# The expert loop of a two-layer MoE trunk: engine order written out by hand, gated values turned earlier, three overflow blocks taken into the loop

## The chip, the cores and the metric

The kernel runs on one core of one Trainium2 chip. The metric is the device time of one execution in microseconds (us). A core has TensorE (PE, matmuls; PEld is its weight load), VectorE (DVE), ScalarE (ACT), GpSimd (POOL) and SyncE (SP, which here issues DMAs), and 16 DMA engines that the queues of all engines share. Each engine takes its instructions strictly in the order of its own list; between engines there are semaphores.

## The reference, cut to what matters

The program has two layers. Each layer has attention and a recurrent mix, and then a mixture of experts: every token picks one of four groups and two of eight experts in it. Of the 1024 tokens, 2048 (token, expert) pairs go to 32 experts, in blocks of 128 rows of one expert.

```python
def block_mlp(args):
    tok, e = args
    xb = h_pad[tok]
    hid = jax.nn.silu(xb @ w_gate[e]) * (xb @ w_up[e])
    return hid @ w_down[e]

yb = lax.map(block_mlp, (row_tok.reshape(n_blocks, ROW_BLOCK), block_e))
y = jax.ops.segment_sum(yb.reshape(R, D) * row_w[:, None], row_tok, num_segments=T + 1)
```

D is 1024 and an expert is 256 wide. All is float32.

## The kernel before, in words

A layer ends with the expert stage, `moe`. Expert e has a fixed block of 128 slots, whose tokens stand in the tables `idx_g` (which row to gather) and `idx_s` (where to scatter); `wsl` holds the weights of the slots. Tokens beyond 128 of one expert go to up to 15 overflow blocks, which `route_overflow` numbers at run time: `ovf` holds how many there are and whose expert each is. With these inputs each layer has three.

For one expert the steps are:

- `gather` (L1595): an indirect DMA, issued by POOL, brings the block's rows from `h2d` into `xg`, of which there are two.
- `transposed` (L1603): eight PE transposes turn them into `xT_ps`; `prepare` splits that into `xT_hi` (ACT, L1611) and `xT_lo` (DVE, L1612), whose sum is the float32 value.
- `load_gu` brings the gate and up weights from HBM in two halves of 1 MB into five buffers `w_gu`; `split_half` splits each half into `w_hi` (ACT, L1580) and `w_lo` (DVE, L1581), three pairs of buffers. `load_d` brings `w_d`, 1 MB, three buffers. All these loads are issued by SP, in order.
- `up` (L1628 to L1630): 24 matmuls into `h_ps`; `hidden` makes the gated values `th` (ACT tanh L1618, DVE L1619 and L1620).
- `down`: two PE transposes turn `th` into `hT_ps` (L1649), a DVE copy brings them back (L1651), four float32 matmuls make `y_ps` (L1655; the profile has each as two), DVE scales them into `yo` (L1658; one buffer), and POOL issues an indirect DMA that scatters `yo` into `yd` (L1659).

`down` of expert e-1 is written behind `up` of e, so that its inputs are ready. The order on each engine is not the order of the code: a scheduler lays the instructions out by the dependencies and its own estimates of time, engine by engine.

After the 32 experts come the overflow blocks, each inside a nested `If` on the count: `prepare_late` and `up_late` (L1642) take the float32 weights without a split, with half as many, slower matmuls. After the last scatter the next layer (or the end) reads `yd` back.

Of the kernel before, what the change touches and what calls it, by code (L numbers as in the profile page):

```python
# [52 lines left out]
class Trunk:  # L53
# [1436 lines left out]
    def route_overflow(self, w, psum):  # L1490
# [83 lines left out]

    def split_half(self, n, eng=None):

        nc = self.nc
        raw = self.raw[n % 5]
        lo, hi = self.parts[n % 3]
        nc.scalar.copy(hi, raw)  # L1580
        (eng or nc.vector).tensor_tensor(lo, raw, hi.bitcast(F32), op=OP.subtract)  # L1581

    def moe(self, l, side, psum):

        nc, tc = self.nc, self.tc
        with ExitStack() as s:
# [28 lines left out]
            def hidden(ph):  # L1615
                x = tx.tile([128, 512], F32, name="th", tag="mt")
                th = x[:, 0:256]
# [3 lines left out]
                return x  # L1621

            def up(e, x):
                hi, lo = x
                ph = psum.tile([128, 512], F32, name="h_ps", tag="h", bufs=2)
                for k in range(NK):
                    wlo, whi = self.parts[(2 * e + k // 4) % 3]
# [3 lines left out]
                return hidden(ph)  # L1631

            def prepare_late(e):
                pt = transposed(e)
                nc.scalar.copy(late[e % 2], pt)
                return late[e % 2]

            def up_late(e, x):

                ph = psum.tile([128, 512], F32, name="h_ps", tag="h", bufs=2)  # L1640
                for k in range(NK):
                    nc.tensor.matmul(ph, x[:, k, :], self.raw[(2 * e + k // 4) % 5][:, k % 4, :], start=(k == 0), stop=(k == NK - 1))  # L1642
                return hidden(ph)

            def down(e, th):
                w = self.wd[e % 3]
                pt = psum.tile([128, 2, 128], F32, name="hT_ps", tag="hT", bufs=1)
                for k in range(2):
                    nc.tensor.transpose(pt[:, k, :], th[:, 128 * k:128 * k + 128], self.ident)  # L1649
                hT = th[:, 256:512].rearrange("p (a b) -> p a b", a=2)  # L1650
                nc.vector.tensor_copy(hT, pt)  # L1651
                po = psum.tile([128, D], F32, name="y_ps", tag="y", bufs=1)
                for half in range(2):
                    for k in range(2):
                        nc.tensor.matmul(po[:, 512 * half:512 * half + 512], hT[:, k, :], w[:, k, 512 * half:512 * half + 512],  # L1655
                                         start=(k == 0), stop=(k == 1))
                yo = tx.tile([128, D], F32, name="yo", tag="x", bufs=1)
                nc.vector.scalar_tensor_tensor(yo, po, self.wsl[:, e:e + 1], gt2, op0=OP.mult, op1=OP.mult)  # L1658
                st = nc.gpsimd.indirect_dma_start(out=self.yd, out_offset=bass.IndirectOffsetOnAxis(ap=self.idx_s[:, e:e + 1], axis=0),  # L1659
                                                  in_=yo, in_offset=None, bounds_check=2 * T - 1, oob_is_err=False)  # L1660
                for o in scat:
                    tc.declare_no_dep(st.ins, o.ins, reason="every slot holds another row")
                scat.append(st)
# [242 lines left out]
```

## Time and profile before

| | us |
|---|---|
| median of 3 runs (2875.5 to 2880.1) | 2878.36 |
| the profiled execution | 2890.55 |
| its span, first to last instruction | 2888.7 |
| PE matmuls busy in the span | 2452.3 (85%) |
| DVE busy | 1845.5 (64%) |
| ACT busy | 1063.5 (37%) |
| POOL busy | 721.3 (25%) |

A window over one turn of the loop tells how much of it each engine works; the timeline gives every instruction's start and duration, with the idle time of its engine before it and what ended that; the DMA views count the packets of a queue in a stretch of time (q0 holds what POOL issues: the gathers and scatters; q1 the loads of SP). PEclk is the share of TensorE's clock that was granted: 1.00 is 2.4 GHz, 0.50 is 1.2 GHz.

### The profile page before, as it was taken

What the parts mean: (1) busy time and instruction counts of PE and PEld (TensorE: products, weight loads), DVE (VectorE), ACT (ScalarE), POOL (GpSimd) and SP (SyncE); (2) the same over time, 40 slices, a digit from 0 to 9 for tenths busy, and PEclk for the clock granted to TensorE, in tenths of its full rate; (3) what the DMA queues carried; (4) which work ended last, traced back from release to release, by engine and by line L of the source; (5) the groups of instructions that cost most, each with busy time, mean ns of one, the idle gap of its engine ahead of it and who ended that gap; (6) DMA issues with size and microseconds to landing.
All of it is one profiled execution on the core that took longest, in us unless ns stands there. A gap on an engine that the chain in (4) does not pass through costs nothing.

```text
span 2888.7 us, 45371 instructions
## 1 busy us (share of the span) xinstructions
PE 2452.3 (85%) x17281; PEld 1842.3 (64%) x17281; DVE 1845.5 (64%) x3927; ACT 1063.5 (37%) x1908; POOL 721.3 (25%) x569
## 2 busy tenths in 40 slices
PE   5999987998789779999849888889877986999991
PEld 3766666787678656666427666778756775666650
DVE  5358785555684767767264689756467566776745
ACT  3333332343463224444133343334345331444421
POOL 4122232222420511111141222221242032111113
PEclk8989998998899779999969989899889986999996
DMA  8477575452442359899551434453443224998874
GB/s 285 157 233 215 178 239 135 134 147 93 161 127 93 140 190 328 312 329 336 188 203 52 136 122 140 151 155 115 127 158 114 98 100 147 342 350 317 306 261 186
DMA packets 264230, 548.99 MB, mean 190 GB/s; under 512 B 77048, under 2 KB 181440, under 8 KB 233280
## 3 DMA queue, kind: packets, MB, share of 16 engines
q1 hardware_dynamic: 235424, 490.90, 50.6%
q0 software_dynamic: 23952, 40.99, 3.9%
q10 hardware_dynamic: 4624, 14.06, 1.2%
q8 instruction: 141, 2.31, 0.3%
q14 instruction: 89, 0.73, 0.1%
HBM read 467.68 MB, written 120.09 MB: 203 GB/s over the span
## 4 chain that ended last, share of the span: by engine, by line
PE 52%; DVE 23%; DMA 11%; ACT 7%; issue 5%; POOL 1%; SPq 1%; DVEq 0%; ACTq 0%; POOLq 0%
PE y_ps L1655 8%; PE pj L335 5%; PE pj L336 5%; PE pj L337 5%; DVE w_lo L1581 4%; ACT w_hi L1580 4%; PE h_ps L1629 3%; PE h_ps L1628 2%; DVE sv_m L724 2%; DVE sv_t L726 2%; PE h_ps L1630 2%; PE po L1284 2%; DMA ada_w<-in_ada_w 2%; DMA yd<-yo,idx_s 2%; PE po L1285 2%
## 5 line engine op out<-in xcount | busy, mean ns | idle before, releaser
L1581 DVE TENSOR_TENSOR w_lo<-w_gu,w_hi 128x2048 fp32r<-128x2048 f32 x122 | 279.6, 2292 | 206.3 <-ACT w_hi L1580 202.1
L1580 ACT CAST w_hi<-w_gu 128x2048 fp32r<-128x2048 f32 x128 | 244.0, 1908 | 384.6 <-PE h_ps L1629 367.4
L335 PE MATMUL pj<-hh,wa_hi 128*128 128x512 f32 x800 | 341.6, 427 | 2.7 <-ACT wa_hi L322 1.9
L336 PE MATMUL pj<-hl,wa_hi 128*128 128x512 f32 x800 | 332.0, 415 | 1.1 <-DVE hl L312 1.1
L337 PE MATMUL pj<-hh,wa_lo 128*128 128x512 f32 x800 | 328.9, 413 | 3.3 <-POOL wa_lo L323 3.3
L1655 PE MATMUL y_ps<-w_d,th 128*128 128x512 f32 x560 | 260.3, 608 | 40.9 <-DVE th L1651 25.5
L1628 PE MATMUL h_ps<-w_hi,xT_hi 128*128 128x512 f32 x512 | 225.8, 441 | 3.9 <-ACT xT_hi L1611 3.9
L1629 PE MATMUL h_ps<-w_hi,xT_lo 128*128 128x512 f32 x512 | 210.8, 412 | 2.6 <-DVE xT_lo L1612 2.6
L1630 PE MATMUL h_ps<-w_lo,xT_hi 128*128 128x512 f32 x512 | 203.2, 397 | 0.0
L1655 PEld LDWEIGHTS y_ps<-w_d,th 128*128 128x128 f32 x560 | 101.3, 190 | 156.9 <-issue 103.3
L323 POOL TENSOR_TENSOR wa_lo<-wa_raw,wa_hi 128x1024 fp32r<-128x1024 f32 x50 | 122.0, 2441 | 315.6 <-ACT wa_hi L322 262.0
L335 PEld LDWEIGHTS pj<-hh,wa_hi 128*128 128x128 f32 x800 | 157.8, 197 | 42.0 <-issue 7.4
L337 PEld LDWEIGHTS pj<-hh,wa_lo 128*128 128x128 f32 x800 | 156.8, 196 | 39.5 <-POOL wa_lo L323 4.6
L336 PEld LDWEIGHTS pj<-hl,wa_hi 128*128 128x128 f32 x800 | 157.8, 197 | 37.2 <-issue 4.5
L1659 POOL DMA_INDIRECT yd<-yo,idx_s x70 | 70.5, 1008 | 402.2 <-DVE yo L1658 323.6
L1595 POOL DMA_INDIRECT xg<-h2d,idx_g x74 | 80.1, 1082 | 299.2 <-PE hT_ps L1649 250.7
L1629 PEld LDWEIGHTS h_ps<-w_hi,xT_lo 128*128 128x128 f32 x512 | 98.2, 192 | 50.5 <-DVE xT_lo L1612 30.9
L1658 DVE SCALAR_TENSOR_TENSOR yo<-y_ps,wsl,gt 128x1024 f32<-128x1024 f32 x70 | 89.5, 1279 | 52.2 <-PE y_ps L1655 27.0
L1628 PEld LDWEIGHTS h_ps<-w_hi,xT_hi 128*128 128x128 f32 x512 | 98.4, 192 | 36.7 <-issue 12.9
L724 DVE TENSOR_TENSOR sv_m<-sv_t,sv_n 64x31 f32<-64x31 f32 (+15 forms) x248 | 104.5, 421 | 23.0 <-DMA sv_n<-sp_z 18.5
L1154 ACT ACTIVATE at_p<-at_s,at_mx 128x256 f32<-128x256 f32 (+7 forms) x128 | 94.9, 742 | 63.7 <-DVE at_mx L1152 63.2
L1152 DVE TENSOR_REDUCE at_mx<-at_s 128x1 f32<-128x256 f32 (+7 forms) x128 | 95.8, 753 | 31.3 <-PE at_s L1150 30.4
(438 smaller groups left out, 5428.7 us busy)
## 6 DMA issues: line engine op xcount, KB each, us to landing
w_gu<-in_moe_w_gu SPq DMA_DIRECT2D x144, 1024.0 KB
w_d<-in_moe_w_down SPq DMA_DIRECT2D x72, 1024.0 KB
ada_w<-in_ada_w SPq DMA_DIRECT2D x80, 512.0 KB
wa_raw<-in_w_in SPq DMA_DIRECT2D x50, 512.0 KB
sp_z<-z SPq DMA_DIRECT2D x32, 768.0 KB
b_zz<-sp_z SPq DMA_DIRECT2D x32, 512.0 KB
cy<-yd SPq DMA_DIRECT2D x16, 1024.0 KB
qkv<-qst SPq DMA_DIRECT2D x48, 256.0 KB
```

Source lines behind the costliest of these rows:

```text
L323: nc.gpsimd.tensor_tensor(lo, raw, hi.bitcast(F32), op=OP.subtract)
L335: nc.tensor.matmul(ps, hi[:, k, :], self.hh[k][:, sl], start=(k == 0), stop=False)
L336: nc.tensor.matmul(ps, hi[:, k, :], self.hl[k][:, sl], start=False, stop=False)
L337: nc.tensor.matmul(ps, lo[:, k, :], self.hh[k][:, sl], start=False, stop=(k == NK - 1))
L724: eng.tensor_tensor(t3, tt[:, 0:j + 1, j].unsqueeze(2).to_broadcast([64, j + 1, 31 - j]), nt[:, j, j + 1:32].unsqueeze(1).to_broadcast([64 ...
L1152: nc.vector.tensor_reduce(mx, ps[:, 0:n], axis=AX.X, op=OP.max, negate=True)
L1580: nc.scalar.copy(hi, raw)
L1581: (eng or nc.vector).tensor_tensor(lo, raw, hi.bitcast(F32), op=OP.subtract)
L1628: nc.tensor.matmul(ph, hi[:, k, :], whi[:, k % 4, :], start=(k == 0), stop=False)
L1629: nc.tensor.matmul(ph, lo[:, k, :], whi[:, k % 4, :], start=False, stop=False)
L1630: nc.tensor.matmul(ph, hi[:, k, :], wlo[:, k % 4, :], start=False, stop=(k == NK - 1))
L1655: nc.tensor.matmul(po[:, 512 * half:512 * half + 512], hT[:, k, :], w[:, k, 512 * half:512 * half + 512], start=(k == 0), stop=(k == 1))
```

## The change

The loop runs over N = 35 blocks: 32 experts and the first three overflow blocks, whose expert SP reads from `ovf`; they are split like the others. Only the fourth and later overflow blocks stay in `If`s.

The loop is written in two pieces, and a new `in_order` ties every instruction of PE, ACT, DVE and POOL in them to the one before it on its engine. So the code's order is the engines' order. SP is left out of it.

The turning of `th` is a step of its own, `turned`. It stands ahead of the transposes of the next expert's rows, and its copy is on ACT, into a tile `hT` of its own. The scatter of e-1 is written ahead of the gather of e+2.

`route_overflow` and the late blocks take their scratch tile from one that an earlier stage (`sg`) uses, `load_gu` loads one half a call, and the buffers of the halves are numbered through.

```diff
+    MORE_E = 3
...
+    @contextmanager
+    def in_order(self, last):
+
+        engines = [e.engine for e in (self.nc.tensor, self.nc.scalar, self.nc.vector, self.nc.gpsimd)]
+        traced = self.nc.cur_bb.bb.instructions
+        n = len(traced)
+        yield
+        for i in traced[n:]:
+            if i.engine in engines:
+                if i.engine in last:
+                    self.tc.add_manual_dep(i, last[i.engine].name, mybir.DependencyInfo(mybir.DependencyClass.NoSync, mybir.DependencyReason.DATA),
+                                           reason="program order")
+                last[i.engine] = i
...
-    def load_gu(self, l, i, e):
-
-        for half in range(2):
-            self.nc.sync.dma_start(self.raw[(2 * i + half) % 5], self.expert_source(l, e, "moe_w_gu")[half])
+    def load_gu(self, l, n, e):
+
+        self.nc.sync.dma_start(self.raw[n % self.RAW], self.expert_source(l, e, "moe_w_gu")[n % 2])
...
-            def down(e, th):
-                w = self.wd[e % 3]
+            def turned(e):
                 pt = psum.tile([128, 2, 128], F32, name="hT_ps", tag="hT", bufs=1)
                 for k in range(2):
-                    nc.tensor.transpose(pt[:, k, :], th[:, 128 * k:128 * k + 128], self.ident)
-                hT = th[:, 256:512].rearrange("p (a b) -> p a b", a=2)
-                nc.vector.tensor_copy(hT, pt)
+                    nc.tensor.transpose(pt[:, k, :], ths[:, e % 2, 128 * k:128 * k + 128], self.ident)
+                nc.scalar.copy(hT, pt)
...
             gather(0)
             gather(1)
-            x, prev = prepare(0), None
-            for e in range(32):
-                th = up(e, x)
-                for n in (2 * e + 3, 2 * e + 4):
-                    if n < 64:
-                        self.split_half(n)
-                if e + 1 < 32:
-                    if e + 2 < 32:
-                        gather(e + 2)
-                    x = prepare(e + 1)
+            x, last = prepare(0), {}
+            for e in range(N):
+                with self.in_order(last):
+                    ph = up(e, x)
+                    if e + 1 < N:
+                        self.split_half(2 * e + 3)
+                    if e:
+                        turned(e - 1)
+                    if e + 1 < N:
+                        x = prepare(e + 1)
+                    hidden(e, ph)
                 if e == 0:
                     nc.sync.dma_start(gt2, self.mod_row(l, 5).partition_broadcast(128))
-                if prev is not None:
-                    down(*prev)
-                prev = (e, th)
-                if e < 28:
-                    self.load_gu(l, e + 4, e + 4)
-                if 0 < e < 30:
-                    self.load_d(l, e + 2, e + 2)
+                with self.in_order(last):
+                    if e:
+                        down(e - 1)
+                        scatter(e - 1)
+                    if e + 2 < N:
+                        gather(e + 2)
+                        self.split_half(2 * e + 4)
+                for n in (2 * e + 8, 2 * e + 9):
+                    if n < 2 * N:
+                        self.load_gu(l, n, expert(n // 2))
+                if e and e + 2 < N:
+                    self.load_d(l, e + 2, expert(e + 2))
                 if e == 2:
                     self.route_overflow(xp, psum)
-                if e == 29:
-                    self.load_gu(l, 32, block_weights(0))
...
+            turned(N - 1)
+            down(N - 1)
+            scatter(N - 1)
...
             with ExitStack() as ifs:
-                for b in range(15):
+                for b in range(self.MORE_E, 15):
                     ifs.enter_context(tc.If(n > b))
...
```

What this does to the engines' lists shows best on POOL, at the start of layer 0's loop, from the first gather on. `xg0` and `xg1` are the two row buffers, so the gathers alternate between them; a row with `yd0` is a scatter. Before:

```order
L1595 DMA xg0_10477<-h2d0_614,idx_g_10451 128x1024
L1595 DMA xg1_10478<-h2d0_614,idx_g_10451 128x1024
L1595 DMA xg0_10477<-h2d0_614,idx_g_10451 128x1024
L1595 DMA xg1_10478<-h2d0_614,idx_g_10451 128x1024
L1595 DMA xg0_10477<-h2d0_614,idx_g_10451 128x1024
L1659 DMA yd0_615<-yo_10610,idx_s_10450 2048x1024
L1595 DMA xg1_10478<-h2d0_614,idx_g_10451 128x1024
L1659 DMA yd0_615<-yo_10676,idx_s_10450 2048x1024
L1595 DMA xg0_10477<-h2d0_614,idx_g_10451 128x1024
```

And now, the same place on POOL:

```order
L1614 DMA xg0_10477<-h2d0_614,idx_g_10451 128x1024
L1614 DMA xg1_10478<-h2d0_614,idx_g_10451 128x1024
L1614 DMA xg0_10477<-h2d0_614,idx_g_10451 128x1024
L1676 DMA yd0_615<-yo_10605,idx_s_10450 2048x1024
L1614 DMA xg1_10478<-h2d0_614,idx_g_10451 128x1024
L1676 DMA yd0_615<-yo_10670,idx_s_10450 2048x1024
L1614 DMA xg0_10477<-h2d0_614,idx_g_10451 128x1024
L1676 DMA yd0_615<-yo_10827,idx_s_10450 2048x1024
L1614 DMA xg1_10478<-h2d0_614,idx_g_10451 128x1024
```

Five gathers stood ahead of the first scatter, and now three: each gather has moved behind two scatters.

On PE, between two experts in the middle of the loop (the last of one `h_ps`, the turnings, `y_ps`, the first of the next `h_ps`), before:

```order
L1629 MATMUL h_ps_11899<-w_hi2_10323,xT_lo_11879 128x512
L1630 MATMUL h_ps_11899<-w_lo2_10322,xT_hi_11878 128x512
L1603 MATMUL xT_ps_11935<-ident_86,xg1_10478 128x128 x8
L1649 MATMUL hT_ps_11948<-ident_86,th_11858 128x128 x2
L1655 MATMUL y_ps_11952<-w_d1_10469,th_11858 128x512 x4
L1628 MATMUL h_ps_11965<-w_hi0_10327,xT_hi_11944 128x512
```

The same place on PE now:

```order
L1647 MATMUL h_ps_11880<-w_hi2_10326,xT_lo_11856 128x512
L1648 MATMUL h_ps_11880<-w_lo2_10327,xT_hi_11855 128x512
L1666 MATMUL hT_ps_11907<-ident_86,th_10481 128x128 x2
L1622 MATMUL xT_ps_11911<-ident_86,xg1_10478 128x128 x8
L1687 MATMUL y_ps_11927<-w_d1_10469,hT_10482 128x512 x4
L1646 MATMUL h_ps_11945<-w_hi0_10322,xT_hi_11920 128x512
```

The two turnings have changed places; `y_ps` stands behind both, as before.

On DVE, from one scaling of `y_ps` to the next, before:

```order
L1658 SCALAR_TENSOR_TENSOR yo<-y_ps,wsl,gt_10476 128x1024
L1581 TENSOR_TENSOR w_lo_10322<-w_gu_10330,w_hi_10323 128x2048
L1651 COPY th<-hT_ps 128x256
L1581 TENSOR_TENSOR w_lo_10326<-w_gu_9795,w_hi_10327 128x2048
L1619 SCALAR_TENSOR_TENSOR th<-th,h_ps 128x256
L1612 TENSOR_TENSOR xT_lo<-xT_ps,xT_hi 128x1024
L1620 TENSOR_TENSOR th<-th,h_ps 128x256
L1658 SCALAR_TENSOR_TENSOR yo<-y_ps,wsl,gt_10476 128x1024
```

And now:

```order
L1673 SCALAR_TENSOR_TENSOR yo<-y_ps,wsl,gt_10476 128x1024
L1595 TENSOR_TENSOR w_lo_10325<-w_gu_10329,w_hi_10324 128x2048
L1595 TENSOR_TENSOR w_lo_10327<-w_gu_10330,w_hi_10326 128x2048
L1631 TENSOR_TENSOR xT_lo<-xT_ps,xT_hi 128x1024
L1637 SCALAR_TENSOR_TENSOR th<-th,h_ps 128x256
L1638 TENSOR_TENSOR th<-th,h_ps 128x256
L1673 SCALAR_TENSOR_TENSOR yo<-y_ps,wsl,gt_10476 128x1024
```

The copy between the two `w_lo` is gone from DVE, and `xT_lo` stands ahead of both steps of `th`.

## Rows read from the trace of the kernel before

**Rows 1.** The page's chain that ended last, by line: shares of the span.

```profile
PE y_ps L1655 8%; PE pj L335 5%; PE pj L336 5%; PE pj L337 5%; DVE w_lo L1581 4%; ACT w_hi L1580 4%; PE h_ps L1629 3%; PE h_ps L1628 2%; DVE sv_m L724 2%; DVE sv_t L726 2%; PE h_ps L1630 2%; PE po L1284 2%; DMA ada_w<-in_ada_w 2%; DMA yd<-yo,idx_s 2%; PE po L1285 2%
```

**Rows 2.** Window, one turn: length, busy PE PEld DVE ACT POOL, PEclk, DMA share, GB/s.

```profile
1261.27:1272.34 11.07, 10.45 (x44) 7.02 (x43) 7.91 (x8) 5.00 (x4) 2.08 (x2) 1.00 0.89 304
```

**Rows 3.** Timeline, that turn: start, duration, instruction, [idle before <-what ended it].

```profile
1261.30 0.79 PE L1628 MATMUL h_ps<-w_hi,xT_hi 128*128 128x512 f32 x1
...
1267.35 1.03 PE L1603 MATMUL xT_ps<-ident,xg 128*128 128x128 f32 x8
...
1268.66 1.07 POOL L1595 DMA_INDIRECT xg<-h2d,idx_g  x1 [3.90 <-PE hT_ps L1649]
...
1269.23 3.70 PE L1655 MATMUL y_ps<-w_d,th 128*128 128x512 f32 x8 [0.62 <-DVE th L1651]
1269.26 2.29 DVE L1581 TENSOR_TENSOR w_lo<-w_gu,w_hi 128x2048 fp32r<-128x2048 f32 x1
...
1274.82 1.01 POOL L1659 DMA_INDIRECT yd<-yo,idx_s  x1 [5.09 <-DVE yo L1658]
```

**Rows 4.** Timeline, the ends of both layers' expert stages.

```profile
1034.22 0.79 PE L1628 MATMUL h_ps<-w_hi,xT_hi 128*128 128x512 f32 x1
...
1058.21 3.70 PE L1655 MATMUL y_ps<-w_d,th 128*128 128x512 f32 x8 [0.38 <-DVE th L1651]
...
1438.21 3.70 PE L1655 MATMUL y_ps<-w_d,th 128*128 128x512 f32 x8 [0.52 <-DVE th L1651]
...
2427.10 0.80 PE L1628 MATMUL h_ps<-w_hi,xT_hi 128*128 128x512 f32 x1
...
2827.61 3.70 PE L1655 MATMUL y_ps<-w_d,th 128*128 128x512 f32 x8 [0.52 <-DVE th L1651]
```

**Rows 5.** Timeline, overflow blocks of layer 0.

```profile
1412.28 3.70 PE L1655 MATMUL y_ps<-w_d,th 128*128 128x512 f32 x8 [0.52 <-DVE th L1651]
...
1416.02 1.28 DVE L1658 SCALAR_TENSOR_TENSOR yo<-y_ps,wsl,gt 128x1024 f32<-128x1024 f32 x1 [3.79 <-PE y_ps L1655]
1417.58 0.99 POOL L1659 DMA_INDIRECT yd<-yo,idx_s  x1 [9.67 <-DVE yo L1658]
1418.88 1.03 POOL L1595 DMA_INDIRECT xg<-h2d,idx_g  x1 [0.31 <-issue]
1419.44 0.33 SPq L1570 DMA_DIRECT2D w_gu<-in_moe_w_gu  x1
1419.97 0.33 SPq L1573 DMA_DIRECT2D w_d<-in_moe_w_down  x1
...
1431.85 1.03 POOL L1595 DMA_INDIRECT xg<-h2d,idx_g  x1 [0.31 <-issue]
```

**Rows 6.** DMA queue q0 from 1432.9 to 1434: packets, MB, share of 16 engines.

```profile
q0 software_dynamic: 144, 0.00, 5.7%
```

**Rows 7.** Timeline, two more gathers and a `y_ps` behind a wait.

```profile
1025.89 1.92 POOL L1595 DMA_INDIRECT xg<-h2d,idx_g  x1 [0.30 <-issue]
...
1397.61 5.40 PE L1655 MATMUL y_ps<-w_d,th 128*128 128x512 f32 x8 [3.48 <-DVE th L1651]
...
1406.87 1.04 POOL L1595 DMA_INDIRECT xg<-h2d,idx_g  x1 [0.30 <-issue]
```

**Rows 8.** DMA queue q0 from 1024.0 to 1031.2.

```profile
q0 software_dynamic: 288, 0.80, 38.8%
```

**Rows 9.** DMA queue q0 from 1422.4 to 1424.6.

```profile
q0 software_dynamic: 144, 0.00, 3.7%
```

**Rows 10.** DMA queue q0 from 1410.9 to 1415.0.

```profile
q0 software_dynamic: 144, 0.02, 2.9%
```

**Rows 11.** Windows: length, busy PE PEld DVE ACT POOL, PEclk, DMA share, GB/s.

```profile
1043.40:1046.70 3.30, 1.59 (x10) 1.06 (x8) 3.03 (x3) 2.61 (x3) 1.03 (x1) 1.00 0.37 84
1046.80:1053.50 6.70, 5.27 (x13) 4.17 (x14) 2.54 (x6) 0.00 (x0) 0.00 (x0) 0.50 0.68 273
...
1398.30:1401.70 3.40, 3.40 (x6) 1.33 (x5) 0.00 (x0) 0.00 (x0) 0.20 (x1) 0.50 0.99 366
```

More of the change, by code (lines that the diff above doesn't have):

```diff
@@ L1556, in first_tiles @@
         self.wd = [wp.tile([128, 2, D], F32, name="w_d0")]
+    RAW = 5
     def more_tiles(self, wp):
-        self.parts = [[wp.tile([128, 4, 512], F32R, name=f"w_{n}{i}") for n in ("lo", "hi")] for i in (2, 1, 0)][::-1]
-        self.raw += [wp.tile([128, 4, 512], F32, name=f"w_gu{i}") for i in range(2, 5)]
+        self.parts = [[wp.tile([128, 4, 512], F32R, name=f"w_{n}{i}") for n in ("hi", "lo")] for i in range(3)]
+        self.raw += [wp.tile([128, 4, 512], F32, name=f"w_gu{i}") for i in range(2, self.RAW)]
     def expert_source(self, l, e, n):
@@ L1591, in moe @@
                 nc.gpsimd.memset(x, 0.0)
+            ths = tx.tile([128, 2, 256], F32, name="th", tag="mt")
+            hT = tx.tile([128, 2, 128], F32, name="hT", tag="mt")
             scat = []
@@ L1641, in up_late, with scaled, scatter, down @@
                 for k in range(NK):
-                    nc.tensor.matmul(ph, x[:, k, :], self.raw[(2 * e + k // 4) % 5][:, k % 4, :], start=(k == 0), stop=(k == NK - 1))
-                return hidden(ph)
-            def down(e, th):
-                w = self.wd[e % 3]
+                    nc.tensor.matmul(ph, x[:, k, :], self.raw[(2 * e + k // 4) % self.RAW][:, k % 4, :], start=(k == 0), stop=(k == NK - 1))
+                hidden(e, ph)
+            def turned(e):
                 pt = psum.tile([128, 2, 128], F32, name="hT_ps", tag="hT", bufs=1)
                 for k in range(2):
-                    nc.tensor.transpose(pt[:, k, :], th[:, 128 * k:128 * k + 128], self.ident)
-                hT = th[:, 256:512].rearrange("p (a b) -> p a b", a=2)
-                nc.vector.tensor_copy(hT, pt)
+                    nc.tensor.transpose(pt[:, k, :], ths[:, e % 2, 128 * k:128 * k + 128], self.ident)
+                nc.scalar.copy(hT, pt)
+            yos = {}
+            def scaled(e, po):
+                yo = yos[e] = tx.tile([128, D], F32, name="yo", tag="x", bufs=1)
+                nc.vector.scalar_tensor_tensor(yo, po, self.wsl[:, e:e + 1], gt2, op0=OP.mult, op1=OP.mult)
+            def scatter(e):
+                st = nc.gpsimd.indirect_dma_start(out=self.yd, out_offset=bass.IndirectOffsetOnAxis(ap=self.idx_s[:, e:e + 1], axis=0),
+                                                  in_=yos.pop(e), in_offset=None, bounds_check=2 * T - 1, oob_is_err=False)
+                for o in scat:
+                    tc.declare_no_dep(st.ins, o.ins, reason="every slot holds another row")
+                scat.append(st)
+            def down(e):
+                w = self.wd[e % 3]
                 po = psum.tile([128, D], F32, name="y_ps", tag="y", bufs=1)
@@ L1656, in down @@
                                          start=(k == 0), stop=(k == 1))
[L1657 to L1663, printed above, removed]
+                scaled(e, po)
             def block_weights(b):
@@ L1705, in moe @@
+            down(N - 1)
+            scatter(N - 1)
+            late = self.lay.tile([128, 8, 128], F32, name="xT", tag="sg")
             n = nc.values_load(self.ovf[0:1, 0:1], min_val=0, max_val=15)
             with ExitStack() as ifs:
[L1707 removed]
+                for b in range(self.MORE_E, 15):
                     ifs.enter_context(tc.If(n > b))
[L1709 to L1710 removed]
+                    if b == self.MORE_E:
+                        gather(32 + b)
+                        overflow(b)
+                    x = prepare_late(32 + b)
@@ L1711, in moe @@
                     if b + 1 < 15:
+                        gather(33 + b)
                         overflow(b + 1)
-                    down(32 + b, up_late(32 + b, x))
-                    if b + 1 < 15:
-                        x = prepare_late(33 + b)
+                    up_late(32 + b, x)
+                    turned(32 + b)
+                    down(32 + b)
+                    scatter(32 + b)
     def sum_of(self, t, pool):
```

61 lines of the change are left out of this document (29 added, 32 removed).

## The prediction

> **What bounds the kernel now.** First the chain of waits on the page: its largest single entry is `y_ps` on TensorE (PE), the second product of an expert [rows 1]. The change touches only the two expert stages, so the next view is the timeline of one expert in the middle of such a stage. From one expert's first `h_ps` to the next one's it takes 11.07 us, and PE is busy for 10.45 of them at full clock [rows 2]. The idle piece with a name is 0.62 us ahead of `y_ps`: PE waits for the turned gated values, whose copy stands on DVE behind a 2.29 us `w_lo` [rows 3]. So the loop is within 6% of PE's own work, and a better order alone can give at most 0.62 us an expert.
>
> The second thing to see is what lies off the path now. The gather of an expert's rows starts as soon as PE has read its buffer, 6 us ahead of the scatter in this turn, and serves a turning two experts later; GpSimd (POOL) otherwise waits, 5.09 us for `yo` [rows 3]. A gather may thus take 20 us without anybody waiting. Third, the ends: layer 0's stage runs from its first `h_ps` at 1034.22 to its last `y_ps` at 1438.21 + 3.70, 407.7 us; layer 1's from 2427.10 to 2827.61 + 3.70, 404.2 us [rows 4]. Each holds 32 experts and three overflow blocks, 12.97 us apart (1418.88 to 1431.85) [rows 5].
>
> **The change part by part.** *Overflow blocks in the loop.* Three blocks of 12.97 us a layer become three more turns of the loop. If a turn cost 10.45 to 11.07, that would save some 6 to 8 us a layer.
>
> *Turned values first, copied on ACT.* The copy leaves DVE (one instruction an expert) and no longer stands behind `w_lo`; the ten PE transposes now cover it. That removes the 0.62 us. Next in line would be nothing but PE.
>
> *The pinned order on POOL.* This is the term that decides. The change puts the gather of expert e+2 behind the scatter of e-1 and pins that. Before, POOL's order has two more gathers ahead of each scatter: after scatter k comes gather k+5; now it is k+3. What is queued behind the scatter's wait for `yo` is therefore the gather for the very next turning, and PE's order puts that turning (`xT_ps` of e+2) ahead of `y_ps` of e. So a ring closes over one turn: `y_ps` of e-1, `yo`, scatter, gather, landing, `xT_ps`, `y_ps` of e. An overflow block of the kernel before shows its first links back to back [rows 5]: `y_ps` ends at 1415.98, `yo` starts 0.04 later and takes 1.28, 0.28 to the scatter, 0.99 for it, 0.31, 1.03 for the gather's issue. After the landing I add 0.2 for the hand-over (an estimate, as from the end of `h_ps` to ACT), 1.03 for `xT_ps` and 3.70 for `y_ps` [rows 3]. Sum: 0.04 + 1.28 + 0.28 + 0.99 + 0.31 + 1.03 + 0.2 + 1.03 + 3.70 = 8.9 us, plus the landing L, counted from the end of the gather's issue to its last packet.
>
> *The landing.* No row of before has PE waiting for a gather, so L is bounded. The gather issued at 1431.85, with no load beside it and no rows to fetch, has all its 144 packets within 1.1 us after 1432.88: the floor [rows 5, 6]. Two gathers of 0.80 MB together, with no load near, have all their 288 packets by 1031.2, 3.4 us after the second one's issue ends at 1027.81 [rows 7, 8]. The empty gather of 1418.88 is a twin of the first but for a `w_gu` load of 1 MB issued 0.56 us after it and a `w_d` 0.53 us later: its 144 packets come between 1422.4 and 1424.6, 4.7 us after 1419.91 [rows 5, 9]. Another, with a few rows to fetch (0.02 MB) and loads on both sides, is issued from 1406.87 to 1407.91 and has its 144 packets by 1415.0, 7.1 us later [rows 7, 10]. In the changed loop, `w_lo` of 2.29 us follows `yo` on DVE and frees a `w_gu` buffer, and SP has `w_gu` and `w_d` queued on it: `w_gu` is issued 2.2 us after `yo`'s end, the gather 0.28 + 0.99 + 0.31 = 1.6 us after it. That is the row of 1418.88 nearly to a tenth: scatter ahead, `w_gu` 0.6 us behind the gather's start, `w_d` next. I take L = 4.7, with 1.1 and 7.1 as ends. The turn is then 8.9 + 4.7 = 13.6 us.
>
> The Trainium skill, "DMA: Bandwidth & Descriptors", section "Queues, rings and completion order", says that each DMA engine alternates between queues, a whole packet of descriptors at a time. By that rule the gather would wait for one load and never two; the twin agrees, the row of 7.1 us does not, so I keep that end.
>
> *PE's clock.* With 10.45 us of work in 13.6, PE stands idle for 3.15 us in one piece. The nearest row: PE idle for 3.48 us up to 1397.61, after which the granted clock is 0.50 (1.2 GHz) from 1398.3 to 1401.7, and `y_ps` takes 5.40 instead of 3.70 [rows 3, 7, 11]. After a stretch with PE busy 1.59 of 3.30 us the clock was at 0.50 too [rows 11]. `xT_ps` and `y_ps` follow the gap and lie in the ring. I take the row's 1.70 us for each turn; ends 0 and 2.6 (with `xT_ps` at half rate too, +0.9 as an estimate of its doubling). The turn: 15.3 us.
>
> *Nothing on the path.* DVE has room (7.91 of 11.07 busy), and so has ACT with the copy (5.00) [rows 2]. The reads of the block's expert number sit on SP, ahead of loads three turns early. The tile shared with `sg` is free by then. Fewer branches: nothing. At the end of a layer the last `yo` may wait for the scatter ahead of it, 0 to 3 us; neighbours also swap places on POOL and PE in layer 1's earlier stages, which I price at nothing, with 10 us either way.
>
> **The sum.** Up to the end of the first `y_ps` the stage stays as it is: 1058.21 + 3.70 - 1034.22 = 27.7 us [rows 4]. Then 32 turns of P. The last two `y_ps` need no new gather: `h_ps` 1267.35 - 1261.30 = 6.05, then twice 0.85 (turning and copy, from the end of `xT_ps` at 1268.38 to 1269.23) and 3.70, together 15.2 [rows 3]. Both layers: 2 x (27.7 + 32 P + 15.2) - 407.7 - 404.2 = 64 P - 726.1. At P = 15.3: +253 us. The profiled execution took 2890.55 us (span 2888.7), so it would be 3144; it is 12.2 us above the median of the runs, 2878.36, to which I add the same: 3132 us. No change would need P = 11.35, that is L = 2.4.
>
> **The rivals.** *A. The gather never limits (faster).* Decides at L below 1.5: then PE's 10.45 us is the turn, -57 us, 2821. For it: the empty gather alone, 1.1 us. Against: every gather with rows or with a load beside it took over twice that [rows 8 to 10]. 6%.
>
> *B. The gather gets ahead of the load.* Both reach the DMA engines within a few tenths of each other; if the gather is first, L is that of the quiet rows, 3.4, the idle piece is 1.9 us and the clock holds: P = 12.3, +61, 2940. For it: the margin is thin. Against: in the twin the margin is the same and the gather came last, and the slowest of 16 engines counts. 14%. The Trainium skill, same page, section "Anatomy of one DMA — SWDGE (gpsimd) path", gives 2.0 us and a byte at 436e3 a us; for half of a 512 KB gather (an estimate) that is 2.6 us, P = 11.5 and 2889. The quiet row is near it, the twin is not.
>
> *C. The ring as forecast, the clock holds.* P = 13.6, +145, 3023. For it: 3.15 us is a little less than 3.48. Against: the stretch with 1.59 us busy, where less idle time did it [rows 11]. 17%.
>
> *D. A backlog of loads.* L = 7.1 and the clock's 1.7: P = 17.7, +407, 3285. For it: the DMA engines are busy 0.89 of the turn now [rows 2]. Against: a longer turn spreads the same bytes. 6%.
>
> **How the numbers follow.** Forecast 57%; A 6, B 14, C 17, D 6. The range takes in C, most of B and the forecast with a clock term of up to 2.6 and L of 0.6 more (P up to 16.9, +356): 2925 to 3235. It leaves out A, D and a tail of B, some 18%. A change under 0.2% (6 us) can't be told from none: faster 7%, same 2%, slower 91%.
>
> **What would show it.** In the profile after: the turn of the loop, 15.3 us; PE's idle time before `xT_ps`, put down to the gather's DMA, about 3 us for each of some 64 turns; POOL's scatter and gather back to back, 0.31 us apart, and the gather's packets behind those of `w_gu`; the granted clock at 0.50 in part of each turn; no wait ahead of `y_ps` for the copy on ACT; DMA share down to some two thirds. I am wrong if PE's wait before `xT_ps` is short while the turn is long (another ring), or if the turn is below 11.3.

## The result: 3432.6 us, 19% slower, twice the loss that was forecast

| | us | ratio to before, 95% interval |
|---|---|---|
| before, median | 2878.6 | |
| changed, median (3420.9 to 3438.8) | 3432.6 | 1.192, 1.189 to 1.196 |
| span of the profiled execution, before and after | 2888.7, 3429.2 | |
| forecast | 3132, range 2925 to 3235 | |

The sign and the place are as forecast, the size is not: +554 us instead of +253, outside the range. All of it lies in the two expert stages. The timeline gives their first `h_ps` and last `y_ps`:

```profile
1026.76 0.78 PE L1646 MATMUL h_ps<-w_hi,xT_hi 128*128 128x512 f32 x1
...
1699.79 3.67 PE L1687 MATMUL y_ps<-w_d,hT 128*128 128x512 f32 x8 [1.21 <-ACTq L1741]
...
2692.35 0.78 PE L1646 MATMUL h_ps<-w_hi,xT_hi 128*128 128x512 f32 x1
...
3365.56 3.67 PE L1687 MATMUL y_ps<-w_d,hT 128*128 128x512 f32 x8 [1.21 <-ACTq L1741]
```

676.7 and 676.9 us, against 407.7 and 404.2 [rows 4]: +541.7. The spans differ by 540.5, so everything outside the stages moved by 1.2 us in sum. The 64 turns that the prediction counts take 19.95 us on average.

The page's groups, first the costliest idle time (busy, mean ns of one | idle before, what ended it):

```profile
L1622 PE MATMUL xT_ps<-ident,xg 128*128 128x128 f32 x560 | 131.8, 414 | 483.1 <-DMA xg<-h2d,idx_g 483.1
L1676 POOL DMA_INDIRECT yd<-yo,idx_s x70 | 183.7, 2624 | 987.4 <-DVE yo L1673 960.3
L1614 POOL DMA_INDIRECT xg<-h2d,idx_g x70 | 180.0, 2571 | 42.4 <-issue 20.2
```

PE waits 483 us for gathers, which no row of before did: ahead of `xT_ps` in all 64 turns, 7.4 us each on average, and once for the first rows of each layer. And the two issues of POOL take 2.6 us on average, where they took 0.99 and 1.03 [rows 5]. One turn of layer 0 on the timeline, as the answer to [rows 3]:

```profile
1302.29 4.62 PE L1687 MATMUL y_ps<-w_d,hT 128*128 128x512 f32 x8
1306.95 1.28 DVE L1673 SCALAR_TENSOR_TENSOR yo<-y_ps,wsl,gt 128x1024 f32<-128x1024 f32 x1 [1.36 <-PE y_ps L1687]
1308.15 2.28 DVE L1595 TENSOR_TENSOR w_lo<-w_gu,w_hi 128x2048 fp32r<-128x2048 f32 x1
1308.51 2.79 POOL L1676 DMA_INDIRECT yd<-yo,idx_s  x1 [14.80 <-DVE yo L1673]
1310.46 3.59 SPq L1586 DMA_DIRECT2D w_gu<-in_moe_w_gu  x2
1311.40 2.29 DVE L1595 TENSOR_TENSOR w_lo<-w_gu,w_hi 128x2048 fp32r<-128x2048 f32 x1 [0.97 <-ACT w_hi L1594]
1311.61 2.97 POOL L1614 DMA_INDIRECT xg<-h2d,idx_g  x1 [0.30 <-issue]
...
1320.17 1.94 PE L1622 MATMUL xT_ps<-ident,xg 128*128 128x128 f32 x8 [7.58 <-DMA xg<-h2d,idx_g]
1321.90 5.05 PE L1687 MATMUL y_ps<-w_d,hT 128*128 128x512 f32 x8
```

This is the forecast ring, link by link, from the end of one `y_ps` at 1306.91 to the next at 1326.95: 20.04 us. And the window over it, as the answer to [rows 2]:

```profile
1302.29:1322.33 20.04, 12.46 (x44) 8.67 (x44) 7.75 (x6) 5.56 (x6) 5.76 (x2) 0.76 0.48 169
```

The granted clock is 0.76 on average, where it was 1.00, and the DMA engines are busy 0.48 instead of 0.89. In the 3.3 us behind the wait, the clock is at 0.50:

```profile
1320.20:1323.50 3.30, 3.30 (x10) 2.38 (x11) 0.31 (x1) 1.36 (x3) 0.00 (x0) 0.50 0.00 0
```

The new thing is POOL. The scatter starts 0.36 us after a `w_lo` has started on DVE, and ends 0.87 after that `w_lo` has ended (1311.30 against 1310.43). The gather starts 0.21 after the second `w_lo` and ends 0.89 after its end. It is so with all 119 issues of this kernel that start under a `w_lo`: they end 0.87 to 0.90 us after its end. So the first theory for the missing 300 us: an issue of POOL that starts under a `w_lo` is held until that ends.

### The profile page after: what moved, and what is told of

Same layout as the page of the kernel before. It is cut to its first block, busy times and chain, and to the rows that moved or that the text cites. A ratio compares the mean times of both kernels' runs of the same rounds, so it can differ in the third digit from the quotient of the medians.

```text
span 3429.2 us, 45434 instructions
## 1 busy us (share of the span) xinstructions
PE 2563.5 (75%) x17313; PEld 1936.1 (56%) x17313; DVE 1871.4 (55%) x3875; ACT 1108.9 (32%) x1988; POOL 934.7 (27%) x565
## 4 chain that ended last, share of the span: by engine, by line
issue 35%; PE 32%; DVE 14%; DMA 8%; POOL 7%; ACT 2%; SPq 1%; POOLq 0%; DVEq 0%; ACTq 0%
POOL xg L1614 5%; PE pj L350 4%; PE pj L351 4%; PE pj L352 4%; DVE sv_m L739 2%; PE at_o L1196 2%; DVE sv_t L741 1%; PE po L1299 1%; PE po L1300 1%; PE po L1301 1%; DMA sp_z<-z 1%; DMA xg<-h2d,idx_g 1%; DMA ada_w<-in_ada_w 1%; PE pl L1343 1%; PE rb_y L899 1%
## 5 line engine op out<-in xcount | busy, mean ns | idle before, releaser
L1622 PE MATMUL xT_ps<-ident,xg 128*128 128x128 f32 x560 | 131.8, 414 | 483.1 <-DMA xg<-h2d,idx_g 483.1
L1676 POOL DMA_INDIRECT yd<-yo,idx_s x70 | 183.7, 2624 | 987.4 <-DVE yo L1673 960.3
L1631 DVE TENSOR_TENSOR xT_lo<-xT_ps,xT_hi 128x1024 fp32r<-128x1024 f32 x70 | 85.7, 1224 | 598.9 <-ACT xT_hi L1630 598.9
L1622 PEld LDWEIGHTS xT_ps<-ident,xg 128*128 128x128 f32 x560 | 106.8, 218 | 495.9 <-issue 495.6
L1594 ACT CAST w_hi<-w_gu 128x2048 fp32r<-128x2048 f32 x140 | 266.8, 1907 | 289.7 <-PE h_ps L1647 282.5
L1595 DVE TENSOR_TENSOR w_lo<-w_gu,w_hi 128x2048 fp32r<-128x2048 f32 x134 | 306.6, 2288 | 81.9 <-ACT w_hi L1594 81.9
L1687 PE MATMUL y_ps<-w_d,hT 128*128 128x512 f32 x560 | 341.7, 767 | 3.4 <-ACTq L1741 2.4
L1630 ACT CAST xT_hi<-xT_ps 128x1024 fp32r<-128x1024 f32 x70 | 70.8, 1012 | 614.3 <-PE xT_ps L1622 614.3
L1687 PEld LDWEIGHTS y_ps<-w_d,hT 128*128 128x128 f32 x560 | 141.7, 268 | 160.0 <-issue 155.7
L1614 POOL DMA_INDIRECT xg<-h2d,idx_g x70 | 180.0, 2571 | 42.4 <-issue 20.2
## 6 DMA issues: line engine op xcount, KB each, us to landing
w_gu<-in_moe_w_gu SPq DMA_DIRECT2D x140, 1024.0 KB
w_d<-in_moe_w_down SPq DMA_DIRECT2D x70, 1024.0 KB
cy<-yd SPq DMA_DIRECT2D x16, 1024.0 KB
```

The source lines that it names most:

```text
L1594: self.nc.scalar.copy(hi, raw)
L1595: eng.tensor_tensor(lo, raw, hi.bitcast(F32), op=OP.subtract)
L1614: nc.gpsimd.indirect_dma_start(out=xg[e % 2], out_offset=None, in_=self.h2d, in_offset=bass.IndirectOffsetOnAxis(ap=self.idx_g[:, e:e + 1] ...
L1622: nc.tensor.transpose(pt[:, k, :], x[:, 128 * k:128 * k + 128], self.ident)
```

## Experiments: the links of the ring

The first four runs leave the other parts of the change as they are. e1 opens the ring, e2 to e4 keep it and take one link away. The rival to the ring was that the pinned order of PE, ACT and DVE, or the copy on ACT, makes the turn long.

**e1: the gather ahead of the scatter.**

```diff
+            with self.in_order(last):
+                gather(2)
...
                     if e + 1 < N:
                         x = prepare(e + 1)
+                    if e + 3 < N:
+                        gather(e + 3)
...
                     if e + 2 < N:
-                        gather(e + 2)
                         self.split_half(2 * e + 4)
```

> The changed kernel, but the gather of expert e+3 is issued right behind the turning of e+1, the last reader of its buffer, and so ahead of the scatter of e-1; all else, the pins too, stays. Theory (a ring over POOL: scatter, gather, landing, turning, y_ps): the ring is opened, a turn falls from 20.05 us to PE's own work, 10.5 to 11.1, so 64 turns give back about 64 x 9.3 = 595: 2820 to 2875 us, PE's idle time before xT_ps under 0.5 us a turn, the clock back at 1.00. Rival (the pinned order of PE, DVE and ACT, or the copy on ACT, makes the turn long): POOL's order is not the cause and it stays above 3300, with the idle time moved to another instruction.

Measured: 2878.8 us, ratio 0.999 (0.997 to 1.001). The whole loss is back, with every other edit of the change in place: the ring is the cause. But the time ends 4 us above the range, with nothing gained over the kernel before; the section after this one takes that up.

**e2: no `w_lo` while POOL issues.**

```diff
+            told = tx.tile([128, 2], F32, name="told", tag="told", bufs=1)
+
+            def behind_issue():
+                nc.gpsimd.memset(told[:, 0:1], 0.0)
+                nc.vector.tensor_copy(told[:, 1:2], told[:, 0:1])
...
                         gather(e + 2)
+                        behind_issue()
                         self.split_half(2 * e + 4)
```

> The ring stays. Behind the gather POOL writes one column of a spare tile, which DVE copies ahead of the split of half 2e+4, so that no w_lo runs on DVE while POOL issues the scatter and the gather. Theory (an issue that starts under a w_lo is held until 0.88 us after its end): scatter and gather take 1.0 us each instead of 2.8 and 3.0, 3.75 us less a turn, 20.05 to 16.3: 3190 us; as w_gu is now issued behind the gather, the landing may shorten too, from 5.6 to 3.4 at the least: 14.1 us a turn, 3050. Rival (the issue is long for a reason of its own, such as POOL's queue or the rows that it moves): 2.8 and 3.0 stay and so does the time, 3420 to 3450.

Measured: 3009.8 us, ratio 1.044 (1.041 to 1.048), below even the lower expectation. On the timeline both issues are short, and `w_lo` follows:

```profile
1307.31 1.01 POOL L1681 DMA_INDIRECT yd<-yo,idx_s  x1 [9.54 <-DVE yo L1678]
1308.62 1.01 POOL L1619 DMA_INDIRECT xg<-h2d,idx_g  x1 [0.31 <-PE h_ps L1653]
...
1309.87 4.50 DVE L1595 TENSOR_TENSOR w_lo<-w_gu,w_hi 128x2048 fp32r<-128x2048 f32 x2
1312.19 2.53 SPq L1586 DMA_DIRECT2D w_gu<-in_moe_w_gu  x2
1313.85 1.07 PE L1627 MATMUL xT_ps<-ident,xg 128*128 128x128 f32 x8 [2.31 <-DMA xg<-h2d,idx_g]
```

The theory of the held issue stands. More went with it: `w_gu` is issued behind the gather now, the landing is 4.2 us instead of 5.6 (1309.63 to 1313.85), and with a wait of 2.31 instead of 7.58 `xT_ps` runs at 1.07. On average over the 64 turns a turn falls from 19.95 to 13.44 us. Of these 6.5 us the two issues are 3.45, the landing is 1.54, and `xT_ps` and `y_ps` are 1.52.

**e3: PE busy while it waits.**

```diff
                         turned(e - 1)
+                        po = psum.tile([128, D], F32, name="y_ps", tag="y", bufs=1)
+                        for _ in range(30):
+                            nc.tensor.matmul(po[:, 0:512], x[0][:, 0, :], x[0][:, 0:4, :], start=True, stop=True)
...
-                        down(e - 1)
+                        down(e - 1, po)
```

> The ring stays. Between the turning of th and that of the next rows PE does 30 more matmuls of 128x512, 6.8 us at full clock, into y_ps, whose first real product overwrites them: PE works where it waited. Theory (the idle gap costs clock, 2.2 us a turn in xT_ps and y_ps): granted clock near 1.00 in the loop, xT_ps 1.03 instead of 1.94, y_ps 3.70 instead of 4.6 to 5.05, the turn 17.85: 3290 us, faster with more work. Rival (the clock plays no part in the ring, or falls for another reason): the time stays at 3430, or grows if the fillers outlast the wait.

Measured: 3330.3 us, ratio 1.156 (1.152 to 1.159): 102 us faster with 7 us more work a turn. In windows over the loop the granted clock is 0.98 to 1.00, and both matmul steps are short again:

```profile
1310.18 7.07 PE L1719 MATMUL y_ps<-xT_hi 128*128 128x512 f32 x30
...
1317.91 1.09 PE L1622 MATMUL xT_ps<-ident,xg 128*128 128x128 f32 x8 [0.67 <-DMA xg<-h2d,idx_g]
1318.84 3.60 PE L1688 MATMUL y_ps<-w_d,hT 128*128 128x512 f32 x8
```

The clock term is real: over the 64 turns `xT_ps` and `y_ps` take 4.61 us together instead of 6.72, 2.1 less, where 2.2 was expected. 40 us of the expected 140 are missing. In some turns the fillers outlast the landing, so the time from the end of the gather's issue to `xT_ps` is 0.28 us longer on average, and a turn is 18.10 us instead of 19.95: 64 x 1.85 = 118 us. And the ends of each stage, which lie outside these turns, grow with the fillers, by some 23 us in the two layers.

**e4: no loads in the loop.**

```diff
-                for n in (2 * e + 8, 2 * e + 9):
-                    if n < 2 * N:
-                        self.load_gu(l, n, expert(n // 2))
-                if e and e + 2 < N:
-                    self.load_d(l, e + 2, expert(e + 2))
```

> The ring stays. The loads of w_gu and w_d in the loop are left out, from the fifth expert's and the fourth's on: the experts compute with the weights that lie in the buffers. Theory (of the landing's 5.6 us some 2 are other transfers ahead of the gather's packets): landing 3.4 to 3.7 us, as of the two quiet gathers before, the turn 18.0: 3300 us. Rival (the landing is the gather's own time): 5.6 stays, 3420 to 3440.

Measured: 3212.4 us, ratio 1.115 (1.108 to 1.121), 90 us better than expected. The gather that ends its issue at 1319.09 lands 3.2 us later:

```profile
1316.12 2.97 POOL L1614 DMA_INDIRECT xg<-h2d,idx_g  x1 [0.31 <-issue]
...
1322.29 1.94 PE L1622 MATMUL xT_ps<-ident,xg 128*128 128x128 f32 x8 [5.19 <-DMA xg<-h2d,idx_g]
```

So 2.4 of the 5.6 us are other transfers (on average over the 64 turns 2.8: 3.02 us against 5.82); beside that the granted clock in the loop is 0.83 instead of 0.76. The changed kernel's queues show which: q1 carries the loads, q0 the scatter and the gather, 144 packets each (packets, MB, share of 16 engines). From 1314.6 to 1316, from 1316 to 1317.5, and from 1317.5 to 1319:

```profile
q1 hardware_dynamic: 51, 0.32, 72.4%
q0 software_dynamic: 114, 0.08, 17.3%
...
q1 hardware_dynamic: 77, 0.63, 99.1%
...
q0 software_dynamic: 135, 0.14, 26.5%
q1 hardware_dynamic: 35, 0.16, 25.1%
```

The 30 packets before 1314.6 and these 114 are the scatter's. Then comes a stretch in which the engines move nothing but `w_gu`, and only behind it the gather.

**e12: two links away at once** (e2's and e4's edits together).

> The ring stays, with two of its terms taken away together: w_lo waits until POOL has issued scatter and gather, and the loads of w_gu and w_d in the loop are left out (the experts compute with the weights that lie in the buffers). Theory (the turn is the sum of the ring's links, each as it was measured by itself): 0.04 + 1.28 + 0.28 + 1.01 + 0.31 + 1.02 + 3.1 for the landing without loads + 1.06 + 3.60 = 11.7 us a turn, PE's gap under 2 us, the clock near 1.00: 1.4 to 1.6 us less a turn than with the quiet issue alone, 2905 to 2925. Rival (the two terms overlap, for instance because the landing waits for the same port): no more than one of them, 3000 or above.

Measured: 2885.9 us, ratio 1.001 (0.999 to 1.003). The turn is the sum of its links: from one `xT_ps` to the next it is 11.74 us, and 11.62 on average over the 64 turns; 11.7 was expected.

```profile
1204.39 1.06 PE L1627 MATMUL xT_ps<-ident,xg 128*128 128x128 f32 x8 [1.29 <-DMA xg<-h2d,idx_g]
...
1216.13 1.06 PE L1627 MATMUL xT_ps<-ident,xg 128*128 128x128 f32 x8 [1.42 <-DMA xg<-h2d,idx_g]
```

The time is 19 us below the range because I subtracted about 1.5 us a turn from e2, whose 64 turns take 13.44 on average: the difference is 1.8. With short issues, no loads in the way and the clock at 1.00 in the loop, the whole kernel takes as long as the one before, though the ring is still closed.

**e7: POOL's order alone, in the kernel before.**

```diff
-                    if e + 2 < 32:
-                        gather(e + 2)
                     x = prepare(e + 1)
...
-                if prev is not None:
-                    down(*prev)
+                with self.in_order(last):
+                    if prev is not None:
+                        down(*prev)
+                    if e + 2 < 32:
+                        gather(e + 2)
```

(`in_order` is taken over with POOL alone in its list.)

> The kernel before, with one part of the change alone: the gather of e+2 is written behind the scatter of e-1 and POOL's order is pinned; overflow blocks, copy on DVE and the scheduler's order of the other engines stay. Theory (this order is the loss, whatever the rest does): PE waits for xg ahead of xT_ps in nearly every turn, and the 32 experts of a layer take 13.6 us a turn if no w_lo lies over POOL's issues (3030), up to 20 if it does (3430): 3030 to 3430. Rival (the loss needs the pinned PE and DVE as well, the scheduler finds another order around it): within 1% of the kernel before.

Measured: 3025.6 us, ratio 1.051 (1.047 to 1.054). The order alone loses 143 us, but not in the way that was expected. `xT_ps` waits little for `xg`; the list of PE's waits (us in total, times, longest) shows the loss elsewhere:

```profile
PE y_ps L1669 <- DVE th L1665: 56.1, 66, 1.5
PE h_ps L1642 <- ACT xT_hi L1625: 30.7, 22, 2.1
PE h_ps L1643 <- DVE xT_lo L1626: 27.6, 24, 2.2
PE xT_ps L1617 <- DMA xg<-h2d,idx_g: 23.6, 10, 3.1
```

These four are 92 us more than in the kernel before, and the `h_ps` matmuls take 35 us more, at a lower granted clock behind such waits (0.55 from 1236.5 to 1243.6): together 127 of the 140 us by which the two stages are longer. Left free on PE, ACT and DVE, the scheduler puts some of the `xT_ps` behind a `y_ps` (on the timeline `y_ps` at 1219.02, `xT_ps` at 1222.56), so that `y_ps` does not wait for the gather there, and others right ahead of `h_ps` (at 1233.44), which then waits for the split of the rows. POOL's issues are mostly short, 1.4 and 1.3 us on average. POOL's order alone is a loss, but the 554 us came only with PE's order, `xT_ps` ahead of `y_ps`, and DVE's, `w_lo` behind `yo`, pinned as well; no run adds these one at a time.

**e11: POOL left out of the pin.** One name less in the list of the changed kernel's `in_order`.

```diff
-        engines = [e.engine for e in (self.nc.tensor, self.nc.scalar, self.nc.vector, self.nc.gpsimd)]
+        engines = [e.engine for e in (self.nc.tensor, self.nc.scalar, self.nc.vector)]
```

> The changed kernel with POOL left out of the pinned order, one name less in a list: PE, ACT and DVE stay pinned, and the scheduler puts two more gathers ahead of the first scatter, as in the kernel before. Theory (POOL's order alone makes the loss; the pins of the others do not): as the early gather, a turn of 11.0 us set by the one yo buffer, 2865 to 2890, ratio 0.995 to 1.003. Rival (the pins of PE, DVE and ACT have a part in the loss of 554 us): above 2950.

Measured: 2875.2 us, ratio 0.998 (0.995 to 1.000). As expected: the pins of the three other engines have no part in the loss once POOL is free.

## Experiments: what is left once the ring is open

With the early gather (e1) the 64 turns take 11.25 us on average, not PE's 10.45. The timeline:

```profile
1306.15 1.28 DVE L1673 SCALAR_TENSOR_TENSOR yo<-y_ps,wsl,gt 128x1024 f32<-128x1024 f32 x1 [3.40 <-DMA yd<-yo,idx_s]
1307.35 4.48 DVE L1595 TENSOR_TENSOR w_lo<-w_gu,w_hi 128x2048 fp32r<-128x2048 f32 x2
1307.71 2.80 POOL L1676 DMA_INDIRECT yd<-yo,idx_s  x1 [5.99 <-DVE yo L1673]
1310.82 1.91 POOL L1614 DMA_INDIRECT xg<-h2d,idx_g  x1 [0.30 <-issue]
1311.75 1.22 DVE L1631 TENSOR_TENSOR xT_lo<-xT_ps,xT_hi 128x1024 fp32r<-128x1024 f32 x1
1313.03 0.50 PE L1647 MATMUL h_ps<-w_hi,xT_lo 128*128 128x512 f32 x1 [0.73 <-DVE xT_lo L1631]
...
1317.30 1.28 DVE L1673 SCALAR_TENSOR_TENSOR yo<-y_ps,wsl,gt 128x1024 f32<-128x1024 f32 x1 [3.54 <-DMA yd<-yo,idx_s]
```

A second ring: there is one buffer for `yo`, so `yo` waits 3.4 us for the scatter before it to land, and the scatter's issue is again held by `w_lo`. What is late next is `xT_lo`, behind `yo` and two `w_lo` on DVE, and PE waits for that. Two cures:

**e5: the scatter's issue kept clear of `w_lo`.** e1 with `behind_issue()` of e2, called behind `scatter(e - 1)`.

> The kernel with the early gather, and in it the w_lo that follows yo on DVE waits until POOL has issued the scatter (a column written by POOL and copied by DVE, as before). Theory (what keeps the early gather at 11.0 us a turn is a second ring over the one yo buffer: yo 1.28, 0.28, a scatter's issue of 2.80 held by w_lo, a landing of 6.8, the next yo; 11.15 in all): with the issue at 1.0 the ring is 9.35, below PE's 10.45, the wait of yo for the scatter (216 us in all) nearly goes, the turn is 10.5 to 10.7: 64 x 0.3 to 0.5 = 20 to 32 us less, 2847 to 2860, a ratio of 0.988 to 0.993 to the kernel before. Rival (the 11.0 come from something else, such as the two w_lo ahead of xT_lo on DVE, which now start 1.3 us later): no faster than the early gather alone, ratio 0.999 or more.

**e6: a second buffer for `yo`.**

```diff
-                yo = yos[e] = tx.tile([128, D], F32, name="yo", tag="x", bufs=1)
+                if e % 2 and 4 < e < N:
+                    yo = yos[e] = self.lay.tile([128, D], F32, name="yo", tag="sg")
+                else:
+                    yo = yos[e] = tx.tile([128, D], F32, name="yo", tag="x", bufs=1)
```

> The kernel with the early gather, and a second buffer for yo: odd experts from the fifth on put it into the tile that the overflow tables used; w_lo follows yo as before. Theory (a ring over the one yo buffer, as for the run with the quiet issue): the ring has two turns to close, yo starts 0.04 us after y_ps, though the scatter's issue is still held at 2.8: turn 10.5 to 10.7, 2847 to 2860, ratio 0.988 to 0.993. Rival (DVE's order, two w_lo ahead of xT_lo): the wait of h_ps for xT_lo stays at 0.7 us or more a turn, ratio 0.997 or more.

**e9: both.**

> Early gather, two buffers for yo, and the scatter's issue kept clear of w_lo, all three. If the ring over yo is what is left of the turn, either of the two cures is enough and both together add nothing: 2847 to 2860, as each alone. If each takes away only a part, this one is the fastest, at PE's own 10.45 a turn: 2835 to 2847, ratio 0.984 to 0.988. Against it: the wait for POOL starts w_lo 1.3 us later on DVE in each turn.

Measured: e5 2807.1 us, ratio 0.976 (0.973 to 0.979); e6 2800.3, 0.972 (0.969 to 0.974); e9 2800.1, 0.972 (0.970 to 0.974). All three beat both kernels. The theory of the ring over `yo` stands, and both cures together add nothing to e6, as it says. All three are faster than expected, because e1's turns were 11.25 us and not the 11.0 that I started from, and because PE's own turn in this order is not 10.45 but 10.02 us. A window of e6:

```profile
1200.00:1300.00 100.00, 100.00 (x421) 70.60 (x420) 77.27 (x61) 53.55 (x51) 36.72 (x20) 1.00 0.98 363
```

PE never stands, and the DMA engines are busy 0.98. Of two parts of the change I measured the worth in that kernel:

**e8: the overflow blocks back in their `If`s** (e6 with `MORE_E = 0`).

> The kernel with the early gather and two buffers for yo, but all overflow blocks stay behind the loop in their Ifs, three a layer. Each turn that leaves the loop gives back 10.02 us and each block costs at least the 12.97 us that it took in the kernel before, more where its gather is not ahead of it: 6 x 3 = 18 to 6 x 10 = 60 us more, 2818 to 2860. Rival (the blocks are worth nothing in the loop): 2800 to 2806.

Measured: 2851.0 us, 51 more than e6, some 25 a layer. That is more than the 6 to 8 us that the prediction gave them, but the blocks written here are also slower than before's 12.97 us: late in layer 0 two `y_ps` of such blocks lie 16.96 us apart.

**e10: the copy of the turned values on DVE** (e6 with `nc.vector.tensor_copy(hT, pt)`).

> The kernel with the early gather and two buffers for yo, but the copy of the turned values is made by DVE again, in its place in the written order. Theory (the copy on ACT is what takes 0.6 us a turn off PE's wait): in that kernel DVE's second w_lo ends 1.1 us after the turning, so the copy ends 1.5 us after it, and y_ps starts 0.9 us later a turn: 64 x 0.9 = 58 us, 2858. Rival (the eight transposes of the next rows cover the copy wherever it is made): 2800 to 2806.

Measured: 2852.3 us, 52 more than e6: a turn takes 10.9 us instead of 10.02. The old wait is back, the same 0.62 us as in [rows 3]:

```profile
1204.34 0.42 DVE L1667 COPY hT<-hT_ps 128x256 f32<-128x256 f32 x1
...
1204.81 3.70 PE L1690 MATMUL y_ps<-w_d,hT 128*128 128x512 f32 x8 [0.62 <-DVE hT L1667]
```

## Why the prediction was right and wrong

| link of the ring, us | forecast | in the turn shown | mean of the 64 turns |
|---|---|---|---|
| `y_ps` end to `yo`, `yo`, to the scatter | 0.04 + 1.28 + 0.28 | 0.04 + 1.28 + 0.28 | 0.04 + 1.28 + 0.30 |
| scatter's issue | 0.99 | 2.79 | 2.78 |
| to the gather | 0.31 | 0.31 | 0.31 |
| gather's issue | 1.03 | 2.97 | 2.70 |
| landing and hand-over | 4.7 + 0.2 | 5.59 | 5.82 |
| `xT_ps` and `y_ps`, with the clock term | 1.03 + 3.70 + 1.70 | 1.73 + 5.05 | 1.73 + 4.99 |
| turn | 15.3 | 20.04 | 19.95 |

- **The mechanism was right.** The ring over POOL was named with all its links in their order, and the result has them; e1 and e11 open it and the loss is gone. PE's wait stands where it was forecast, in each of the 64 turns. The gather's packets come behind those of `w_gu`, the clock falls to 0.50 behind the wait, and in none of the 64 turns does `y_ps` wait for the copy on ACT.
- **The step that failed is the two issues of POOL.** I took 0.99 and 1.03 from an overflow block [rows 5], in which DVE does nothing beside them. In the loop a `w_lo` follows `yo` on DVE; the prediction itself says so, to place the load of `w_gu`, and asks no further. On average they are 2.78 and 2.70, together 3.46 us a turn too small; over 64 turns 221 us, nearly three quarters of the 301 us between forecast and result. e2 shows it directly: with no `w_lo` beside them both are back at 1.0.
- **The trace of before had the clue.** The gather of [rows 7] that took 1.92 us was an outlier that the prediction used for its landing and not for its length. Beside it DVE ran a product of the routing with two tiles as inputs, which ends at 1026.93; the gather ends 0.88 after that, at 1027.81. And the plain turn has it too, with a `w_lo`:

```profile
1026.26 0.67 DVE L1525 TENSOR_TENSOR ro_big<-r_oh,ro_os 128x512 f32<-128x512 f32 x1
...
1266.55 2.29 DVE L1581 TENSOR_TENSOR w_lo<-w_gu,w_hi 128x2048 fp32r<-128x2048 f32 x1 [3.07 <-ACT w_hi L1580]
```

  The `w_lo` ends at 1268.84; the gather of [rows 3] starts at 1268.66 and ends 0.89 after that end, at 1269.73. It was held for 0.18 us, just little enough to look like nothing.
- **The landing** with its hand-over is 0.69 us longer than forecast in this turn, 0.92 on average. The twin in [rows 9] had `w_gu` issued behind the gather; with the gather held, the first `w_gu` is issued 4 us ahead of the end of its issue. This error follows from the first: in e2, where the issues are short and `w_gu` comes behind the gather again, it is 4.28 on average, less than forecast.
- **The clock term** was 1.70 and is 2.05 in this turn, 1.99 on average: the row that it came from had a gap of 3.48 us, this turn has one of 7.58. The DMA share, forecast at two thirds, is 0.48 because the same bytes are spread over a longer turn.
- **Luck** kept the error from being larger. In e2, whose issues have the forecast length, a turn is 13.44 us and not 15.3: the wait is 2.4 us on average, and `xT_ps` and `y_ps` take 5.20 us behind it, 0.47 more than the 4.73 of [rows 3] and not 1.70. As far as e2 stands for the turn that was forecast, the clock term in it was too large, and made up for a part of the issues.
- **The sum** was 64 P less a constant. With P = 19.95 it gives 64 x 19.95 - 726 = +551, where the two stages are 541.7 us longer: the formula held within 10 us, its P did not.
- **The range** ended at 3235, since it took all bounds from the landing and the clock and none from the issues. Rival D had a longer turn for another reason and was too short as well. Rival A, the loop at PE's own pace, was priced at 2821. With the gather off the path (e1 and e11) the time is 2879 and 2875, because the second ring limits it then; PE's own pace (e6) is 2800.
- **What was priced at nothing** outside the loop was so here: the rest of the program moved by 1.2 us in sum. But "next in line would be nothing but PE" was wrong: e1 shows a second ring over `yo` that the prediction did not look for.

## What to carry to other kernels

An order that is pinned on one engine's queue can close a ring through engines that it doesn't touch: follow what is queued behind each waiting instruction until it comes back, and cost the ring's links with the neighbours that they will have, not with those of a quiet row. When an issue on POOL lies in such a ring, look at what DVE runs at that moment, and keep the issues of the next inputs ahead of anything that waits for this turn's result. Once a ring is open, look for the next one at the buffer of which there is only one.

## What the hardware showed

- An indirect DMA's issue on POOL that starts under a `w_lo` (both inputs in SBUF) ends 0.87 to 0.90 us after it, in all 119 cases of the changed kernel: up to 3.01 us instead of 1.0. An issue that starts a moment earlier goes through in 1.0, in nine cases by 0.04 us or less, and `w_lo` takes at most 2.32 us then. Here it is 0.03 us, in an early turn of the changed kernel:

```profile
1092.50 1.01 POOL L1614 DMA_INDIRECT xg<-h2d,idx_g  x1 [0.31 <-issue]
...
1092.53 2.30 DVE L1595 TENSOR_TENSOR w_lo<-w_gu,w_hi 128x2048 fp32r<-128x2048 f32 x1 [1.02 <-ACT w_hi L1594]
```

  `xT_lo`, whose first input is in PSUM, does not hold an issue. In e7 this scatter starts under one, 0.75 us before its end, and takes the plain 1.02:

```profile
1429.73 1.23 DVE L1626 TENSOR_TENSOR xT_lo<-xT_ps,xT_hi 128x1024 fp32r<-128x1024 f32 x1 [0.30 <-ACT xT_hi L1625]
1430.21 1.02 POOL L1673 DMA_INDIRECT yd<-yo,idx_s  x1 [0.31 <-issue]
```

  The Trainium skill, "SBUF — State Buffer", section "Who interferes with whom", says that a DVE instruction with two SBUF inputs contends with a GpSimd instruction that reads SBUF; the trace agrees, if the issue reads its indices there, which no run here shows by itself.
- PE idle for 7.4 us of each 20 us turn, on average, had a granted clock of 0.76 in the loop; 7 us of useless matmuls in that gap brought it to 0.98 to 1.00 and made the kernel 102 us faster (e3).
- A gather of 128 rows is there for PE 3.0 us after its issue without loads beside it (e4, 1.3 to 3.8), 4.3 with loads issued behind it (e2, 2.3 to 7.6), and 5.8 with a load issued ahead of it (the changed kernel, 2.2 to 7.6). These are means over the 64 turns, in the last of which no load is left.
